# Windowed attention beside a weight projection: units in column order, other load distances, gate stores on ScalarE's queue

## The chip, the cores and the metric

The kernel runs on one core of a Trainium2 chip. The metric is the time on the device in microseconds (us). Five engines work in it: TensorE (PE, with PEld for the loading of the stationary operand), VectorE (DVE), ScalarE (ACT), GpSimd (POOL) and SyncE (SP). DMAs are issued by instructions in the streams of SP, ACT and POOL, and a stream is in order: an instruction that waits holds all behind it.

## The reference

One layer of a hybrid encoder, 1024 tokens (a grid of 16 rows by 64 columns) of 1024 channels, all in float32. What matters here is the middle of it:

```python
h = h + 0.5 * swiglu(rms_norm(h))            # first half of the feed-forward
z = rms_norm(h) @ W_in                       # columns: q | k | v | ssm input | gate_attn | gate_ssm
for every head and every token (r, c):       # attention in a clamped window of 8 rows x 16 columns
    sc = q . k[window] * 64 ** -0.5 + bias[window]
    attn = softmax(sc) @ v[window]
ssm  = bidirectional state-space scan, then a gated linear unit
h = h + (sigmoid(gate_attn) * (attn @ Wa) + sigmoid(gate_ssm) * (ssm @ Ws)) @ W_out
h = h + 0.5 * swiglu(rms_norm(h))            # second half, then an embedding term and a last norm
```

## The kernel before, in words

Every product of float32 matrices is made as three matmuls of high and low parts (`mm3`); `split` makes the parts, the high one with a copy on ScalarE, the low one with a subtraction on VectorE. The large products go by a seven-product scheme of half blocks.

From about 700 us on, after the first feed-forward, the projections of `W_in` are made. Values come first (`values`, results stored to `v_d`), then a loop over `items` (84 of them: twelve column pairs of `W_in`, two for queries and keys in each of four, and eight for gates, seven products each). An item `(n, i)` is four groups of three matmuls (`s_run`), and after each group `tick()` lets a second program advance: the generator `mixer_side()`. So TensorE's order is written out by hand: items, and pieces of the side program between them. The order on the other engines is made by a scheduler from priorities and dependencies.

`s_ahead(n)` loads the weight blocks `LL` items ahead (`s_load`, on ScalarE's queue, line 1506) and makes the operands `LP` = 2 items ahead (`b_operand`, VectorE's sums at line 428 and the split at 159 and 160). `s_evac` (line 1539 and 1543) copies accumulators into `z` tiles or adds to them; `s_out` makes of a finished block either query or key parts (`qkh`, `qkl`, stored by ScalarE's queue to `q_d` and `k_d`) or a gate block, which is stored to `g_d` by GpSimd's queue. The stores are collected in `later` and issued by `s_store` in the next item (line 1549).

The side program's attention is 64 units: eight heads, two halves of the token rows (`rb`), four column blocks (`cb`). In iteration `j` of its loop it makes the scores of unit `j` (`attn_scores`: two matmuls at line 1228, with the query tiles `qh` and `ql` as stationary operand; VectorE adds the bias table `tb`; ScalarE takes the exponential and scales), the transposes of unit `j - 2` (`attn_turn`, line 1244, then `pth` and `ptl`) and the products with the values of unit `j - 4` (`attn_values`, into a PSUM bank `O` that four units share; after the fourth, `ot` at line 1262 goes to `o_d`). Then it yields for three ticks. Two scan steps of the state-space branch go to GpSimd in each iteration (lines 1154 to 1156). All loads of this program are on SP's queue: keys (`load_k`, 1201), queries (`load_q`, 1208), values (`load_v`, 1213), tables (`load_tab`, 1220).

Tiles come from pools with a fixed number of buffers: 24 buffers of 128 x 512 (`tmp`) hold query tiles, `vhl`, `blk`, the parts `wh` and `wl`, `z`, `qkh`, `qkl`, `ot` and `ol` in turn. A new tile waits until the readers of the buffer's former tile are done, a store's landing included. PSUM has eight banks.

After the attention `ssm_out` and the gated unit follow in the side program; `load_br` loads the attention result from `o_d` and splits it for the branch product, and the gates are read back from `g_d` from 1202 us on.

Of the kernel before, what the change touches and what calls it, by code (L numbers as in the profile page):

```python
# [8 lines left out]
F32 = mybir.dt.float32  # L9
# [3 lines left out]
ALU = mybir.AluOpType  # L13
# [28 lines left out]
def encoder_block(ctx, tc, I, out):  # L42
# [1157 lines left out]
        for a, s_ in enumerate(halves2):  # L1200
            nc.sync.dma_start(t[s_].bitcast(F32), k_d[hp, a, halves2[i]])

    def load_q(hd, rb):
        hp, i = hd // 2, hd % 2
        qs[hd, rb] = [tmp("q" + n, dt=F32R) for n in "hl"]
        for a in range(2):
            for s_ in halves2:
                nc.sync.dma_start(qs[hd, rb][a][s_].bitcast(F32), q_d[hp, a, halves2[i], hsl(rb)])

    def load_v(hd, cb):  # L1210
        n = 4 * KNC[cb]
# [10 lines left out]
    def attn_scores(hd, rb, cb):  # L1222
        n = KNC[cb]
        nk = 12 * n
        kv = khl[hd].rearrange("p (r c) -> p r c", c=GRID)[:, 4 * rb:4 * rb + 12, KC0[cb]:KC0[cb] + n]
        s3 = bank("s")[:, 0:nk].rearrange("p (r c) -> p r c", c=n)
        for a in range(2):
            T.matmul(s3, lhsT=qs[hd, rb][a][:, ksl(cb)], rhs=kv, start=a == 0, stop=a == 1)
        sm = ta("sm")[:, 0:nk]
        tab = tabs[2 * hd + rb, KVAR[cb]]  # L1230
        st = ap_.tile([P, 4], F32, tag="stat", bufs=4, name="stat")
        V.tensor_tensor_reduce(out=sm.rearrange("p (r c) -> p r c", c=n), in0=s3,
                               in1=tab.rearrange("p (r c) -> p r c", c=n), scale=-1.0, scalar=3.0e38,
                               op0=ALU.add, op1=ALU.min, accum_out=st[:, 0:1])
        A.activation(sm, sm, AF.Exp, bias=st[:, 0:1], scale=-1.0, accum_out=st[:, 1:2])
        V.reciprocal(st[:, 2:3], st[:, 1:2])
        A.activation(sm, sm, AF.Copy, scale=st[:, 2:3])
        return sm
# [11 lines left out]
    def attn_values(hd, rb, cb, O, ph, pl):  # L1250
        kp = 4 * KNC[cb]
        hl = vld[hd, cb]
        for g in range(3):

            T.matmul(O[:, ksl(cb)], lhsT=hl[0:kp, rb + g], rhs=ph[0:kp, ksl(g)], start=(g == 0), stop=False,
                     skip_group_check=True)
            T.matmul(O[0:64, ksl(cb)], lhsT=hl[0:kp, rb + g, 0:64], rhs=pl[0:kp, ksl(g)], start=False, stop=(g == 2),
                     skip_group_check=True)
        if cb == 3:
            ot, ol = tmp("ot"), tmp("ol")  # L1260
            A.copy(ol[0:64], O[64:128])
            V.tensor_tensor(ot[0:64].rearrange("p (r b c) -> p b r c", r=8, b=4),
                            O[0:64].rearrange("p (b r c) -> p b r c", b=4, r=8),
                            ol[0:64].rearrange("p (b r c) -> p b r c", b=4, r=8), ALU.add)
            late.append((o_d[hd * 64:(hd + 1) * 64, hsl(rb)], ot[0:64]))


    ygs = {}
# [41 lines left out]
    def mixer_side():  # L1310
        yield from u_second()
        while 3 not in stored:
            yield 1
        yield 7
        new_x()
        ld = {}
        for pr in range(3):
            ld[pr] = inject_load(pr)
        yield 10
        for pr in range(NPAIR):  # L1320
            if pr + 3 < NPAIR:
                ld[pr + 3] = inject_load(pr + 3)
            inject(pr, *ld.pop(pr))
            yield 2
        while "v" not in stored:
            scan_steps(1)
            yield 1
        for cb in range(4):
            scan_steps(4)
            yield 4  # L1330
            load_v(0, cb)
        load_tab(0, 0)
        while 0 not in ready:
            scan_steps(1)
            yield 1
        units = [(hd, rb, cb) for hd in range(NH) for rb in range(2) for cb in range(4)]
        n = len(units)
        load_k(0)
        load_q(0, 0)
        for _ in range(6):  # L1340
            scan_steps(1)
            yield 2
        sms, pts, O = {}, {}, {}
        late.clear()
        lo, so = {}, {}
        for j in range(n + 5):
            if j < n:
                hd, rb, cb = units[j]
                b = 2 * hd + rb
                load_tab(b + cb // 2, (1, 2, 0, 0)[cb]) if cb < 3 else None  # L1350
                if cb == 2 and rb == 0:
                    load_q(hd, 1)
                if cb == 2 and rb == 1 and hd + 1 < NH:
                    while hd + 1 not in ready:
                        yield 1
                    load_q(hd + 1, 0)
                if rb == 0 and cb == 2 and hd + 1 in ready:
                    load_k(hd + 1)
                if rb == 1 and cb == 2 and hd + 1 < NH and hd + 1 not in khl:
                    load_k(hd + 1)  # L1360
                sms[j] = attn_scores(hd, rb, cb)
            if 0 <= j - 2 < n:
                pts[j - 2] = attn_turn(units[j - 2][2], sms.pop(j - 2))
            while late:
                nc.scalar.dma_start(*late.pop())
            if 0 <= j - 4 < n:
                hd, rb, cb = units[j - 4]
                if cb == 0:
                    O[hd, rb] = bank("O")
                attn_values(hd, rb, cb, O[hd, rb], *pts.pop(j - 4))  # L1370
                if rb == 1 and hd + 1 < NH:
                    load_v(hd + 1, cb)
            scan_steps(2)
            if j >= n:
                if j - n < 3:
                    lo[j - n] = ssm_load(j - n)
            yield 3
        scan_steps(NCH)
        for p in range(NPAIR + 1):
            if 3 <= p + 3 < NPAIR:  # L1380
                lo[p + 3] = ssm_load(p + 3)
            if p < NPAIR:
                so[p] = ssm_out(p, *lo.pop(p))
            if p > 0:
                so.pop(p - 1)()
            yield 1 + p % 2
        yield 3
        glu_load(0)
        raws = [glu_raw(0), glu_raw(1)]
        yield 11  # L1390
        glu_act(0)
        glu_load(1)
        yield 2
        glu_act(1)
        for t in range(2):
            yield from glu_half(t, raws)
# [61 lines left out]
    def load_br(t, b):  # L1458

        res = []  # L1460
        if b == 0:
            for k in range(0, 4, 2):
                st = tst("br")
                nc.sync.dma_start(st.rearrange("p (k c) -> p k c", k=2),
                                  o_d[k * P:(k + 2) * P, hsl(t)].rearrange("(k p) c -> p k c", p=P))
                for i in range(2):
                    hi, lo = tx("bh"), tx("bl")
                    split(hi, lo, st[:, hsl(i)])
                    res.append((hi, lo))
            return res  # L1470
        for k in range(4):
            st = tmp("br")
            hi, lo = tx("bh"), tx("bl")
            mark["br"] = nc.sync.dma_start(st.rearrange("p (s c) -> p s c", s=L),
                                           y2_d[ksl(k)].rearrange("p (s c) -> p s c", s=L)[:, :, t * 64:(t + 1) * 64]).ins
            sv = st.rearrange("p (s c) -> p c s", s=L)
            hv, lv = (x.rearrange("p (c s) -> p c s", s=L) for x in (hi, lo))
            split(hv, lv, sv)
            res.append((hi, lo))
        return res  # L1480
# [30 lines left out]
    def s_out(n, c, t, second, src):  # L1511
        kind, m = pairs[n]
        if kind == "g":
            if c == "21":
                z, src = tmp("z21"), src
                A.copy(z, src)
                src = z
            later.append((nc.gpsimd, g_d[2 * m + second, :, hsl(t)], src))
            return
        hi, lo = tmp("qkh", dt=F32R), tmp("qkl", dt=F32R)  # L1520
        if second:
            A.activation(hi, src, AF.Copy, scale=0.125)
            V.scalar_tensor_tensor(lo, src, 0.125, hi.bitcast(F32), ALU.mult, ALU.subtract)
        else:
            def view(x):
                return x.rearrange("p (b r c) -> p r b c", b=4, r=8)
            sv = src.rearrange("p (r b c) -> p r b c", r=8, b=4)
            A.copy(view(hi), sv)
            V.tensor_tensor(view(lo), sv, view(hi).bitcast(F32), ALU.subtract)
        for i, x in enumerate((hi, lo)):  # L1530
            later.append((nc.scalar, (k_d if second else q_d)[m, i, :, hsl(t)], x.bitcast(F32)))
# [32 lines left out]
        with tc.high_priority(offset=PRI):  # L1564
            s_evac(n, i)

    LL, LP = 5, 2
    done_ = {"l": 0, "p": 0}

    def s_ahead(n):  # L1570
# [387 lines left out]
```

## Time and profile before

| what | value |
|---|---|
| median of three runs | 2112.91 us (2112.85 to 2114.22) |
| the profiled execution | 2113.88 us |
| its span, first to last instruction | 2112.1 us |
| mean granted clock | 0.992 |
| busy: PE, DVE, ACT, POOL | 2060.9, 1468.4, 1011.0, 480.2 us |
| the 64 attention units | 825.4 to 1061.9 us |

In a row of the timeline stand start, length, engine, line, operation, the tiles written and read by the program's names, and in brackets the idle time before it on its engine and what ended it. SPq, ACTq and POOLq are the DMA issues in those engines' streams; their length is the issue and not the transfer. A row of waits reads: who waited, for what, total us, times, longest. The granted clock is TensorE's as a share of full speed.

### The profile page before, as it was taken

The page shows a single profiled execution, that of the slowest core. Times are in us where ns is not written, and L with a number is a line of the kernel's source. Part 1 is how long each engine was busy: PE and PEld are TensorE (multiplying, and loading weights), DVE is VectorE, ACT ScalarE, POOL GpSimd, SP SyncE. Part 2 cuts the span into 40 slices and gives each one's busy share as a digit, 9 for nine tenths or more (in the row PEclk, how much of TensorE's full clock was granted, in tenths as well). Part 3 has the DMA queues.
Part 4 walks back from the last instruction along what each step waited for, and adds up shares of the span by engine and source line. Part 5 has one row for each costly group of instructions (what it writes and reads, how often), then busy time and mean ns, then how long its engine had stood idle before and what let it go on. Part 6 is the DMA issues. An engine that isn't in the chain of part 4 may idle for free.

```text
span 2112.1 us, 28243 instructions
## 1 busy us (share of the span) xinstructions
PE 2060.9 (98%) x9518; PEld 1685.9 (80%) x9518; DVE 1468.4 (70%) x2478; ACT 1011.0 (48%) x1878; POOL 480.2 (23%) x720
## 2 busy tenths in 40 slices
PE   9999999999999998898999999999999999999998
PEld 3788888888888887777888788788888888888887
DVE  7897776667967847555655669896565665785855
ACT  6434333344445535656655546553333334445544
POOL 0037565540000518888031002000000000000000
PEclk9999999999999999999999999999999999999999
DMA  3434444485543557566675776143323338533302
GB/s 131 142 118 152 129 131 128 139 284 156 185 120 107 149 180 238 171 197 192 192 243 185 231 264 164 65 154 102 123 80 121 99 100 293 170 105 95 115 26 80
DMA packets 212464, 319.75 MB, mean 151 GB/s; under 512 B 37856, under 2 KB 81504, under 8 KB 212320
## 3 DMA queue, kind: packets, MB, share of 16 engines
q1 hardware_dynamic: 173840, 258.14, 38.9%
q10 hardware_dynamic: 31760, 44.07, 6.3%
q0 software_dynamic: 6720, 15.75, 2.6%
q8 instruction: 75, 1.23, 0.2%
q14 instruction: 69, 0.57, 0.1%
HBM read 224.01 MB, written 93.85 MB: 150 GB/s over the span
## 4 chain that ended last, share of the span: by engine, by line
PE 80%; POOL 7%; DVE 5%; DMA 3%; ACT 2%; issue 2%; SPq 0%; ACTq 0%; DVEq 0%; POOLq 0%
PE dx L190 4%; PE dx L191 4%; PE dx L192 4%; PE gx L190 3%; PE ux L190 3%; PE ux L192 3%; PE gx L192 3%; PE gx L191 3%; PE ux L191 3%; POOL sc L1154 3%; PE dy L192 2%; PE dy L190 2%; PE dy L191 2%; POOL X L1156 2%; POOL sc L1155 2%
## 5 line engine op out<-in xcount | busy, mean ns | idle before, releaser
L159 ACT CAST wh<-hbuf 128x512 fp32r<-128x512 f32 x280 | 173.0, 622 | 389.2 <-PE gx L191 84.3
L160 DVE TENSOR_TENSOR wl<-hbuf,wh 128x512 fp32r<-128x512 f32 x280 | 215.4, 772 | 121.7 <-ACT wh L159 119.7
L159 ACT CAST wh<-wblk 128x512 fp32r<-128x512 f32 x190 | 117.9, 622 | 188.7 <-PE dx L191 82.4
L160 DVE TENSOR_TENSOR wl<-wblk,wh 128x512 fp32r<-128x512 f32 x190 | 130.6, 690 | 49.8 <-ACT wh L159 40.2
L190 PE MATMUL dx<-ah,wh 128*128 128x512 f32 x416 | 163.5, 393 | 0.4 <-DVE hbuf L694 0.3
L192 PE MATMUL dx<-ah,wl 128*128 128x512 f32 x416 | 161.9, 389 | 0.0
L191 PE MATMUL dx<-al,wh 128*128 128x512 f32 x416 | 161.9, 389 | 0.0
L160 DVE TENSOR_TENSOR al<-araw,ah 128x512 fp32r<-128x512 f32 x154 | 106.5, 696 | 49.6 <-PE dx L191 21.1
L190 PE MATMUL gx<-xh,wh 128*128 128x512 f32 x320 | 125.0, 391 | 1.3 <-DVE c L581 1.2
L190 PE MATMUL ux<-xh,wh 128*128 128x512 f32 x320 | 125.0, 390 | 0.0
L191 PE MATMUL gx<-xl,wh 128*128 128x512 f32 x320 | 124.5, 389 | 0.0
L192 PE MATMUL ux<-xh,wl 128*128 128x512 f32 x320 | 124.5, 389 | 0.0
L192 PE MATMUL gx<-xh,wl 128*128 128x512 f32 x320 | 124.5, 389 | 0.0
L191 PE MATMUL ux<-xl,wh 128*128 128x512 f32 x320 | 124.5, 389 | 0.0
L159 ACT CAST ah<-araw 128x512 fp32r<-128x512 f32 x154 | 94.9, 619 | 44.5 <-PE dx L191 14.2
L160 DVE TENSOR_TENSOR wl<-blk,wh 128x512 fp32r<-128x512 f32 x84 | 61.4, 733 | 49.6 <-ACT wh L159 47.2
L190 PEld LDWEIGHTS dx<-ah,wh 128*128 128x128 f32 x416 | 78.1, 188 | 18.6 <-DVE hbuf L694 1.2
L191 PEld LDWEIGHTS dx<-al,wh 128*128 128x128 f32 x416 | 78.1, 188 | 16.8 <-issue 0.7
L428 DVE TENSOR_TENSOR hbuf<-hbuf 128x512 f32<-128x512 f32 x120 | 89.7, 749 | 2.1
L192 PEld LDWEIGHTS dx<-ah,wl 128*128 128x128 f32 x416 | 78.1, 188 | 16.3
L1154 POOL TENSOR_TENSOR sc<-X,rho 128x128 f32<-128x128 f32 x128 | 75.5, 590 | 59.4 <-ACT X L1137 49.6
L190 PE MATMUL px<-xh,wh 128*128 128x512 f32 x192 | 80.6, 420 | 6.1 <-ACT z L1539 4.7
(399 smaller groups left out, 5775.6 us busy)
## 6 DMA issues: line engine op xcount, KB each, us to landing
araw<-a_d SPq DMA_DIRECT2D x154, 256.0 KB
a_d<-c SPq DMA_DIRECT2D x148, 256.0 KB
wblk<-in_wd SPq DMA_DIRECT2D x88, 256.0 KB
hbuf<-in_wg SPq DMA_DIRECT2D x40, 512.0 KB
hbuf<-in_wu SPq DMA_DIRECT2D x40, 512.0 KB
blk<-in_win ACTq DMA_DIRECT2D x48, 256.0 KB
hbuf<-in_xT SPq DMA_DIRECT2D x32, 256.0 KB
h_d<-hbuf ACTq DMA_DIRECT2D x32, 256.0 KB
```

The costliest lines, as they stand in the source:

```text
L159: A.copy(hi, src)
L160: return eng.tensor_tensor(lo, src, hi.bitcast(F32), ALU.subtract)
L190: T.matmul(o, lhsT=wh, rhs=xh, start=first, stop=False, skip_group_check=more)
L191: T.matmul(o, lhsT=wh, rhs=xl, start=False, stop=False, skip_group_check=more)
L192: T.matmul(o, lhsT=wl, rhs=xh, start=False, stop=last, skip_group_check=more)
L428: V.tensor_tensor(b11, (b12, b22, None, None, b21)[i - 2], b11, ALU.subtract)
L1154: G.tensor_tensor(sc, both, rho4, ALU.mult)
L1155: G.tensor_tensor(cross1, cross1, cross, ALU.add)
L1156: G.tensor_tensor(x1, sc[:, 0], x1, ALU.add)
```

## The change

The units run in the order head, column block, row half, so that both row halves of a column block follow each other and share the value tile. With it:

- A query tile holds a column pair `cp` of both row halves instead of one row half with all columns; its two runs per partition are 1 KB each instead of one of 2 KB. It is loaded at `u == 1` and `u == 5` of the eight units of a head, three units ahead of its first use; before, two.
- Tables are loaded two units ahead, and three of them ahead of the loop. Keys are asked for where they were, at the third and seventh unit of a head.
- Two value tiles are loaded ahead of the loop, and each further one two column blocks (four units) ahead; before, the four of a head were loaded a whole head ahead.
- The bank `O` holds a head and a column pair; `ot` is written in the bank's own order with no strided view, `o_d` keeps that order within a row half, and the split in `load_br` reorders it with the strided view that `ot` had.
- Gate stores go by `nc.scalar` instead of `nc.gpsimd`.
- `LL` goes from 5 to 4, so weight blocks are loaded four items ahead instead of five.

The numbers of matmuls and of DMAs stay the same.

```diff
-    def load_q(hd, rb):
+    def load_q(hd, cp):
...
-                nc.sync.dma_start(qs[hd, rb][a][s_].bitcast(F32), q_d[hp, a, halves2[i], hsl(rb)])
+                nc.sync.dma_start(qs[hd, cp][a][s_].rearrange("p (t c) -> p t c", t=2).bitcast(F32),
+                                  q_d[hp, a, halves2[i]].rearrange("p (t b c) -> p t b c", t=2, b=2)[:, :, cp])
...
-            T.matmul(s3, lhsT=qs[hd, rb][a][:, ksl(cb)], rhs=kv, start=a == 0, stop=a == 1)
+            T.matmul(s3, lhsT=qs[hd, cb // 2][a][:, ksl(2 * rb + cb % 2)], rhs=kv, start=a == 0, stop=a == 1)
...
-        if cb == 3:
+        if cb % 2 == 1 and rb == 1:
             ot, ol = tmp("ot"), tmp("ol")
             A.copy(ol[0:64], O[64:128])
-            V.tensor_tensor(ot[0:64].rearrange("p (r b c) -> p b r c", r=8, b=4),
-                            O[0:64].rearrange("p (b r c) -> p b r c", b=4, r=8),
-                            ol[0:64].rearrange("p (b r c) -> p b r c", b=4, r=8), ALU.add)
-            late.append((o_d[hd * 64:(hd + 1) * 64, hsl(rb)], ot[0:64]))
+            V.tensor_tensor(ot[0:64], O[0:64], ol[0:64], ALU.add)
+            late.append((o_d[hd * 64:(hd + 1) * 64].rearrange("p (t b c) -> p t b c", t=2, b=2)[:, :, cb // 2],
+                         ot[0:64].rearrange("p (t c) -> p t c", t=2)))
...
-            load_v(0, cb)
+            if cb < 2:
+                load_v(0, cb)
         load_tab(0, 0)
+        load_tab(1, 0)
...
-        units = [(hd, rb, cb) for hd in range(NH) for rb in range(2) for cb in range(4)]
+        units = [(hd, rb, cb) for hd in range(NH) for cb in range(4) for rb in range(2)]
...
-                b = 2 * hd + rb
-                load_tab(b + cb // 2, (1, 2, 0, 0)[cb]) if cb < 3 else None
-                if cb == 2 and rb == 0:
+                u = j % 8
+                if u not in (2, 3):
+                    load_tab(2 * ((j + 2) // 8) + j % 2, KVAR[(j + 2) % 8 // 2])
+                if u == 1:
                     load_q(hd, 1)
-                if cb == 2 and rb == 1 and hd + 1 < NH:
+                if u == 5 and hd + 1 < NH:
                     while hd + 1 not in ready:
                         yield 1
                     load_q(hd + 1, 0)
-                if rb == 0 and cb == 2 and hd + 1 in ready:
+                if u == 2 and hd + 1 in ready:
                     load_k(hd + 1)
-                if rb == 1 and cb == 2 and hd + 1 < NH and hd + 1 not in khl:
+                if u == 6 and hd + 1 < NH and hd + 1 not in khl:
                     load_k(hd + 1)
...
-                attn_values(hd, rb, cb, O[hd, rb], *pts.pop(j - 4))
-                if rb == 1 and hd + 1 < NH:
-                    load_v(hd + 1, cb)
+                attn_values(hd, rb, cb, O[hd], *pts.pop(j - 4))
+                if rb == 1 and (j - 4) // 2 + 2 < 4 * NH:
+                    load_v(((j - 4) // 2 + 2) // 4, ((j - 4) // 2 + 2) % 4)
...
-                    split(hi, lo, st[:, hsl(i)])
+                    sv = st[:, hsl(i)].rearrange("p (b r c) -> p b r c", b=4, r=8)
+                    hv, lv = (x.rearrange("p (r b c) -> p b r c", r=8, b=4) for x in (hi, lo))
+                    split(hv, lv, sv)
...
-            later.append((nc.gpsimd, g_d[2 * m + second, :, hsl(t)], src))
+            later.append((nc.scalar, g_d[2 * m + second, :, hsl(t)], src))
...
-    LL, LP = 5, 2
+    LL, LP = 4, 2
```

The order that comes of it, at three places. First GpSimd's stream of before, where the first gate block, `z12`, is stored among the scan steps (`sc` and `X` are the scan's tiles):

```order
L1154 TENSOR_TENSOR sc_6135<-X_6590,rho_1128 128x128
L1155 TENSOR_TENSOR sc_6135<-sc_6135 128x64
L1156 TENSOR_TENSOR X_6590<-sc_6135,X_6590 128x32x2
L1549 DMA g_d_85<-z12_7910 128x512
L1154 TENSOR_TENSOR sc_6135<-X_6590,rho_1128 128x128
L1155 TENSOR_TENSOR sc_6135<-sc_6135 128x64
```

And the same store in ScalarE's stream of the changed kernel (`blk` is a weight block, `sm` a softmax, `pth` its transpose):

```order
L1545 COPY z12_7910<-px_7716 128x512
L1512 DMA blk_7912<-in_win 128x512
L159 CAST wh_7914<-blk_7765 128x512
L1369 DMA o_d_84<-ot_7898 128x1x256
L1236 ACTIVATE sm_7932,stat_7933<-sm_7932,stat_7933 128x288
L1247 CAST pth_7942<-pt_7938 96x384
L1512 DMA blk_7964<-in_win 128x512
L159 CAST wh_7967<-blk_7515 128x512
L1238 ACTIVATE sm_7932<-sm_7932,stat_7933 128x288
L1555 DMA g_d_85<-z12_7910 128x512
L1247 CAST pth_7998<-pt_7994 96x384
```

The store has left the scan's stream; it now stands nine rows behind the copy that begins its block, with a split, an exponential and transposes of the attention around it.

Second ScalarE's stream at the start of the items, behind the last value stores, before:

```order
L1549 DMA v_d_80<-vs_7132 128x4x128
L1506 DMA blk_7151<-in_win 128x512
L159 CAST wh_7154<-blk_6845 128x512
L159 CAST xh_7189<-s3_7143 128x512
L1539 COPY z11_7183<-px_7158 128x512
L159 CAST wh_7185<-blk_6849 128x512
```

And in the changed kernel:

```order
L1555 DMA v_d_80<-vs_7132 128x4x128
L159 CAST wh_7152<-blk_6845 128x512
L159 CAST xh_7189<-s3_7143 128x512
L1545 COPY z11_7181<-px_7156 128x512
L1512 DMA blk_7183<-in_win 128x512
L159 CAST wh_7185<-blk_7028 128x512
```

The block load has moved from ahead of the first evacuation `z11` to behind it; the cast `wh` still stands ahead.

Third SP's stream at the query load of the 25th unit (the first of head 3; its query tile is `qh_8651` before and `qh_8593` after; `khl_8857` and `khl_8853` are the key tile of head 4), before:

```order
L1213 DMA vhl_8514<-v_d_80 96x1x512
L1220 DMA tb_8543<-in_tabs 128x384
L1220 DMA tb_8595<-in_tabs 128x288
L1220 DMA tb_8649<-in_tabs 128x288
L1201 DMA khl_8857<-k_d_82 64x1024
L1208 DMA qh_8651<-q_d_81 64x512 x2
L1208 DMA ql_8652<-q_d_81 64x512 x2
```

And in the changed kernel:

```order
L1214 DMA vhl_8508<-v_d_80 128x1x512
L1221 DMA tb_8591<-in_tabs 128x288
L1208 DMA qh_8593<-q_d_81 64x2x256 x2
L1208 DMA ql_8594<-q_d_81 64x2x256 x2
L1214 DMA vhl_8622<-v_d_80 128x1x512
L1221 DMA tb_8651<-in_tabs 128x288
L1201 DMA khl_8853<-k_d_82 64x1024
```

The query load has moved ahead of that key load, with a value load ahead of it that stood elsewhere before.

More of the change, by code (lines that the diff above doesn't have):

```diff
@@ L1201, in load_k @@
             nc.sync.dma_start(t[s_].bitcast(F32), k_d[hp, a, halves2[i]])
-    def load_q(hd, rb):
+    def load_q(hd, cp):
         hp, i = hd // 2, hd % 2
-        qs[hd, rb] = [tmp("q" + n, dt=F32R) for n in "hl"]
+        qs[hd, cp] = [tmp("q" + n, dt=F32R) for n in "hl"]
         for a in range(2):
             for s_ in halves2:
-                nc.sync.dma_start(qs[hd, rb][a][s_].bitcast(F32), q_d[hp, a, halves2[i], hsl(rb)])
+                nc.sync.dma_start(qs[hd, cp][a][s_].rearrange("p (t c) -> p t c", t=2).bitcast(F32),
+                                  q_d[hp, a, halves2[i]].rearrange("p (t b c) -> p t b c", t=2, b=2)[:, :, cp])
     def load_v(hd, cb):
@@ L1252, in attn_values @@
         hl = vld[hd, cb]
+        oc = ksl(2 * rb + cb % 2)
         for g in range(3):
-            T.matmul(O[:, ksl(cb)], lhsT=hl[0:kp, rb + g], rhs=ph[0:kp, ksl(g)], start=(g == 0), stop=False,
+            T.matmul(O[:, oc], lhsT=hl[0:kp, rb + g], rhs=ph[0:kp, ksl(g)], start=(g == 0), stop=False,
                      skip_group_check=True)
-            T.matmul(O[0:64, ksl(cb)], lhsT=hl[0:kp, rb + g, 0:64], rhs=pl[0:kp, ksl(g)], start=False, stop=(g == 2),
+            T.matmul(O[0:64, oc], lhsT=hl[0:kp, rb + g, 0:64], rhs=pl[0:kp, ksl(g)], start=False, stop=(g == 2),
                      skip_group_check=True)
-        if cb == 3:
+        if cb % 2 == 1 and rb == 1:
             ot, ol = tmp("ot"), tmp("ol")
             A.copy(ol[0:64], O[64:128])
-            V.tensor_tensor(ot[0:64].rearrange("p (r b c) -> p b r c", r=8, b=4),
-                            O[0:64].rearrange("p (b r c) -> p b r c", b=4, r=8),
-                            ol[0:64].rearrange("p (b r c) -> p b r c", b=4, r=8), ALU.add)
-            late.append((o_d[hd * 64:(hd + 1) * 64, hsl(rb)], ot[0:64]))
+            V.tensor_tensor(ot[0:64], O[0:64], ol[0:64], ALU.add)
+            late.append((o_d[hd * 64:(hd + 1) * 64].rearrange("p (t b c) -> p t b c", t=2, b=2)[:, :, cb // 2],
+                         ot[0:64].rearrange("p (t c) -> p t c", t=2)))
     ygs = {}
@@ L1367, in mixer_side @@
                 hd, rb, cb = units[j - 4]
-                if cb == 0:
-                    O[hd, rb] = bank("O")
-                attn_values(hd, rb, cb, O[hd, rb], *pts.pop(j - 4))
-                if rb == 1 and hd + 1 < NH:
-                    load_v(hd + 1, cb)
+                if cb % 2 == 0 and rb == 0:
+                    O[hd] = bank("O")
+                attn_values(hd, rb, cb, O[hd], *pts.pop(j - 4))
+                if rb == 1 and (j - 4) // 2 + 2 < 4 * NH:
+                    load_v(((j - 4) // 2 + 2) // 4, ((j - 4) // 2 + 2) % 4)
             scan_steps(2)
```

## The prediction

> **What bounds the kernel now.** I read the page first, then a table of engine time by stage, the waits of the attention stage, TensorE's timeline in it, and last the queues that feed it. The page's span and engine row, then the table's row for the attention stage (columns: length; busy time and count of PE, PEld, DVE, ACT, POOL; granted clock; DMA share; GB/s):
>
> ```profile
> span 2112.1 us, 28243 instructions
> PE 2060.9 (98%) x9518; PEld 1685.9 (80%) x9518; DVE 1468.4 (70%) x2478; ACT 1011.0 (48%) x1878; POOL 480.2 (23%) x720
> ...
> 796.00:1062.00 266.00, 241.75 (x1348) 205.27 (x1349) 167.90 (x398) 163.75 (x369) 184.25 (x367) 0.95 0.64 193
> ```
>
> TensorE is busy 98% of the span, so only its idle time and its slow-clock time can be won. Both are in this stage: 266.0 − 241.8 = 24.2 us idle and a granted clock of 0.95, with every other engine below 70% and the DMA engines at 64%. What TensorE, VectorE and the SP queue wait for there, from the list of waits (total us, times, longest):
>
> ```profile
> DVE blk L428 <- DMA blk<-in_win: 11.7, 6, 3.8
> DVE ot L1262 <- DMA g_d<-z: 9.2, 1, 9.2
> PE s L1228 <- DMA qh<-q_d: 8.7, 5, 2.7
> PE s L1228 <- DMA ql<-q_d: 8.4, 7, 3.4
> PE pt L1244 <- ACT sm L1237: 5.5, 1, 5.5
> PE px L190 <- ACT z L1539: 4.7, 3, 3.2
> ...
> SPq L1208 <- DMA g_d<-z: 25.6, 3, 14.7
> SPq L1201 <- DMA k_d<-qkh: 14.3, 3, 8.8
> ```
>
> TensorE waits for query tiles (8.7 + 8.4 = 17.1 us), for one softmax (5.5) and for accumulator evacuations (4.7). The SP queue, which loads the queries, waits three times for gate stores to land. The holes stand in short windows, and in each of them the clock is low too (columns as above):
>
> ```profile
> 792.00:800.00 8.00, 4.82 (x15) 3.60 (x14) 4.76 (x7) 4.70 (x9) 7.06 (x13) 0.79 0.89 291
> 862.00:878.00 16.00, 10.27 (x47) 8.33 (x46) 5.39 (x14) 5.56 (x15) 14.14 (x29) 0.79 0.33 108
> 896.00:906.00 10.00, 7.53 (x34) 5.95 (x32) 4.88 (x11) 4.78 (x11) 8.51 (x20) 0.83 0.59 199
> 914.00:922.00 8.00, 5.50 (x23) 4.33 (x22) 3.24 (x9) 3.99 (x10) 6.82 (x16) 0.79 0.77 222
> 957.00:971.00 14.00, 7.96 (x34) 6.40 (x33) 4.96 (x13) 5.80 (x14) 11.80 (x29) 0.76 0.54 168
> 992.00:1001.00 9.00, 6.08 (x25) 4.74 (x24) 3.90 (x12) 6.15 (x14) 7.54 (x18) 0.81 0.52 170
> ```
>
> The time lost to the clock is (1 − clock) × length: 1.7 us at 792, 3.4 at 862, 1.7 at 896, 1.7 at 914, 3.4 at 957, 1.7 at 992. TensorE's holes and, for the pace, its first and last score row in the stage, from its timeline (start, length, instruction, idle time before it and what ended that):
>
> ```profile
> 796.03 0.80 PE L190 MATMUL px<-xh,wh 128*128 128x512 f32 x1 [3.18 <-ACT z L1539]
> ...
> 825.42 0.29 PE L1228 MATMUL s<-khl,qh 128*128 128x288 f32 x1
> 827.00 0.40 PE L1228 MATMUL s<-khl,ql 128*128 128x288 f32 x1 [1.28 <-DMA ql<-q_d]
> 872.61 0.45 PE L1244 MATMUL pt<-ident,sm 128*96 128x128 f32 x1 [5.47 <-ACT sm L1237]
> 884.77 0.37 PE L1228 MATMUL s<-khl,ql 128*128 128x288 f32 x1 [0.23 <-DMA ql<-q_d]
> 917.13 0.37 PE L1228 MATMUL s<-khl,qh 128*128 128x288 f32 x1 [1.90 <-DMA qh<-q_d]
> 918.10 0.37 PE L1228 MATMUL s<-khl,ql 128*128 128x288 f32 x1 [0.61 <-DMA ql<-q_d]
> 961.31 0.37 PE L1228 MATMUL s<-khl,qh 128*128 128x288 f32 x1 [2.69 <-DMA qh<-q_d]
> 965.02 0.58 PE L1228 MATMUL s<-khl,ql 128*128 128x288 f32 x1 [3.35 <-DMA ql<-q_d]
> 1061.89 0.29 PE L1228 MATMUL s<-khl,qh 128*128 128x288 f32 x1
> ```
>
> Sixty-four units in 1061.9 − 825.4 = 236.5 us are 3.75 us a unit; an item of the weight projections is four ticks and a unit three, so an item takes 5.0 us.
>
> **The change part by part.** All sums are made against the profiled execution, 2113.9 us, which stands 1.0 us above the median of 2112.9.
>
> *Gate stores from GpSimd's queue to ScalarE's.* One store followed from its data to its victims, from the timelines of four engines, and the landing times of all 32 of them:
>
> ```profile
> 852.04 0.69 DVE L1543 TENSOR_TENSOR z<-py,z 128x512 f32<-128x512 f32 x1
> 868.39 0.58 POOL L1549 DMA_DIRECT2D g_d<-z  x1
> 870.80 0.68 DVE L1262 TENSOR_TENSOR ot<-O,ol 64x512 f32<-64x512 f32 x1 [9.20 <-DMA g_d<-z]
> 879.74 1.13 SPq L1208 DMA_DIRECT2D qh<-q_d  x2
> ...
> 953.73 1.48 SPq L1208 DMA_DIRECT2D qh<-q_d  x2
> 961.04 1.08 SPq L1208 DMA_DIRECT2D ql<-q_d  x2
> DMA to landing us min/median/max: 2.3/4.4/6.9
> ```
>
> The gate block was ready at 852.04 + 0.69 = 852.7, but its store was issued at 868.4, 15.7 us later, because GpSimd had scan steps ahead of it; the transfer took about 2.3 us. VectorE's `ot` needed that buffer and stood for 9.20 us with the softmax of the next units queued behind it; that is TensorE's 5.47 us hole at 872.6. The SP queue also waited 14.7 us for a gate store and could not issue the query loads behind it, which gave the 0.23 at 884.8; near 954 the same happened again, and the query loads at 953.7 and 961.0 came so late that TensorE idled 2.69 and 3.35 us. Sum: 5.47 + 0.23 + 2.69 + 3.35 = 11.7 us idle and 3.4 + 3.4 = 6.8 us of clock, 18.5 us in all. On ScalarE a store stands some nine instructions of 0.3 to 0.6 us behind its data. I take −16.7 and leave 1.8 for one store that still lands late; the bounds are −11.7 (holes alone) and −18.5.
>
> The clock loss is put to the holes because it stands in their windows, also after small ones: 1.90 + 0.61 us at 917 were followed by 0.79. The Trainium skill, "TensorE: Matmul & The Clock Gate", section "Why this matters for your kernels", warns of gaps above about 3 us alone; the window at 914 shows the loss with less, so the trace decides against it here. By the page the losses at 896, 914 and 992 would not go with the holes, and the sum would be 2.6 us smaller.
>
> *Queries three units ahead, by column pair.* TensorE's remaining query waits are 17.1 − 6.3 (0.23 + 2.69 + 3.35) − 1.28 (the first unit, whose load is not moved) = 9.5 us, and the clock at 896, 914 and 992 another 5.1: 14.6 us at most. In the order the loads for the hole at 917 no longer stand behind the next head's key load, which waited up to 8.8 us for its stores; that hole (2.51 + 1.7) should go. Elsewhere the loads gain about one unit, 3.75 us, but they also have a values or table load ahead of them that wasn't there. I take half, −7.3; bounds −4.2 and −14.6. Each load now has 1-KB runs in place of 2-KB ones; with the DMA engines at 64% I cost this at nothing.
>
> *The hole at 796.* ScalarE's cast ahead of the evacuation waited for value stores and the block load stood ahead of it:
>
> ```profile
> 794.35 0.62 ACT L159 CAST wh<-blk 128x512 fp32r<-128x512 f32 x1 [3.03 <-DMA v_d<-vs]
> ```
>
> With LL at 4 the block load falls behind the evacuation, but this cast and its wait stay ahead. Of 3.18 + 1.7 = 4.9 us I take −1.0; bounds 0 and −4.9.
>
> *Weight blocks one item later.* VectorE already waited 11.7 us for blocks, in six places; the longest, from ScalarE's issue to VectorE's use, and for scale one pass of the softmax (the group's mean is in ns):
>
> ```profile
> 1017.57 0.33 ACTq L1506 DMA_DIRECT2D blk<-in_win  x1
> 1024.09 0.69 DVE L428 TENSOR_TENSOR blk<-blk 128x512 f32<-128x512 f32 x1 [3.80 <-DMA blk<-in_win]
> ...
> L1235 ACT ACTIVATE sm<-sm,stat 128x288 f32<-128x288 f32 x32 | 17.2, 537 | 7.5 <-DVE stat L1232 5.7 <-DVE qkl L1523 1.2 <-issue 0.4
> ```
>
> None of these reached TensorE. A stall of VectorE delays the softmax queued behind it, and a transpose comes two units (7.5 us) after its scores; with some 3 us for the softmax itself (four passes of about 537 ns and their hand-overs, an estimate from that row) the cover is about 4.5 us. If each wait grew by the whole 5.0 us, the longest would overshoot by 3.8 + 5.0 − 4.5 = 4.3 us and the other five, 1.6 us on average now, by 2.1 each: 14.8 us. If the loads land in time, nothing. I take +3.0, near the lower end, since the nearest row, 3.80, showed nothing on TensorE.
>
> *The rest.* ScalarE gets 32 more issues of 0.33 us (10.6 us over some 320 us, beside an engine 62% busy), and anything that waits there holds its casts and exponentials. Values come two column units ahead in place of a whole head; even the shorter lead, about 8.6 us of matmuls in the order, is above the gate stores' landings of 2.3 to 6.9. Together +1.5; bounds 0 and +6. The 16-element runs move from `ot` to the splits of the attention branch. The rows of one form:
>
> ```profile
> L159 ACT CAST bh<-br 128x512 fp32r<-128x512 f32 x16 | 12.9, 871 | 9.0 <-DMA br<-o_d 9.0
> L1528 ACT CAST qkh<-z 128x512 fp32r<-128x512 f32 x4 | 2.5, 616 | 2.0 <-DVE z L1543 2.0
> ```
>
> The key and query split already has that access pattern and takes 616 ns on ScalarE, so the moved one costs nothing that TensorE sees. Table loads two units ahead and the order of the units change no count; zero, with the query term's bounds for doubt.
>
> Sum: −16.7 − 7.3 − 1.0 + 3.0 + 1.5 = −20.5, so 2093.4 on the profiled scale and **2092.4** on that of the median.
>
> **The rivals.** *Everything comes back*: 18.5 + 14.6 + 2.5 (half of the hole at 796) less 1.5 gives 2112.9 − 34.1 = 2078.8. For it: the new order gives each query load about the same lead. Against: tables, values, keys and queries still share SP's queue.
>
> *The transfers, not the issue, are what is late*: the stores move at an earlier time into the query and block loads, and buffers come free no sooner. Then the first term is nothing and the sum is −7.3 − 1.0 + 4.5 = −3.8, 2109.1. Against it stands 2.3 us of transfer beside 15.7 of waiting for issue. For it: the windows at 792 and 914 show DMA shares of 0.89 and 0.77. The Trainium skill, "DMA: Bandwidth & Descriptors", section "Issuing engines are not separate DMA queues", says that the transfers of all issuing engines interleave on the same DMA engines and another queue saves issue time alone; by that rule this rival would hold wherever issue time was not the loss.
>
> *Slower by the blocks*: the stage has about 266 / 5.0 = 53 items, so 30 block loads at four in seven items. If half stall VectorE 2.1 us beyond the cover and seven of those holes bring a clock loss of 1.7, the cost is 15 × 2.1 + 7 × 1.7 = 43.4 in place of 3.0: 2132.8. It decides against the change once blocks cost about 24 us more than I give, an overshoot of 1.6 us in fifteen places with no clock loss. For it: waits of up to 3.8 us at the old lead. Against: only six of thirty waited at all.
>
> **How the numbers follow.** My forecast has 0.60, full recovery 0.13, late transfers 0.15, blocks 0.12. With the bounds of its terms the forecast's own range is 2083 to 2103. About 0.2%, 4.2 us, is what a measurement of this kernel can tell from no change: 2108.7 is the bound of faster, and late transfers straddle it, so half of their chance and a little more is put to faster: 0.60 + 0.13 + 0.08 = 0.81; the other 0.07 is no change, and blocks are slower, 0.12. The range runs from 2079, which cuts off half of full recovery, to 2110, which leaves out the blocks and the upper edge of late transfers: 0.06 + 0.12 + 0.02.
>
> **What would show it.** In the new profile: SP's waits for `g_d` at L1208 gone and no `ot` waiting for `g_d` (first term); TensorE's waits for `qh` and `ql` below 6 us in all (second); the px hole near 796 still there (third); VectorE's block waits at 15 to 25 us with no TensorE hole behind them (fourth); clock of the stage near 0.98. The prediction is wrong if gate stores on ScalarE's queue stand as long for their data or buffers as on GpSimd's, if the query waits stay at 9 us, or if TensorE's transposes begin to wait for softmax in many places.

## The result, and the profile after

The changed kernel takes 2098.75 us (median of five, 2093.88 to 2104.60) against 2112.91 (2112.82 to 2114.79): ratio 0.9935, 95% interval 0.9913 to 0.9957. That is 14.2 us faster by the medians, where 20.5 were forecast; 2092.4 was predicted, with a range of 2079 to 2110. The runs of the changed kernel spread over 10.7 us, those of before over 2.

The page after, and two rows of the table by stage, the attention stage and what follows it:

```profile
span 2097.0 us, 28186 instructions
PE 2057.4 (98%) x9518; PEld 1681.4 (80%) x9518; DVE 1468.5 (70%) x2478; ACT 1010.1 (48%) x1878; POOL 465.2 (22%) x688
...
796.00:1062.00 266.00, 252.80 (x1462) 214.59 (x1463) 180.46 (x422) 172.88 (x393) 178.60 (x354) 0.99 0.71 209
1062.00:1260.00 198.00, 191.75 (x907) 158.98 (x906) 114.06 (x188) 109.34 (x194) 22.60 (x36) 0.97 0.73 235
```

The second of these rows before:

```profile
1062.00:1260.00 198.00, 191.79 (x956) 160.32 (x955) 114.86 (x195) 110.53 (x201) 29.91 (x50) 1.00 0.73 237
```

The span is 15.1 us shorter. TensorE is busy 2060.9 − 2057.4 = 3.5 us less, as less of its work ran at the low clock, and so idle 11.6 us less. The gain is in the attention stage: in the same 266 us TensorE is busy for 252.8 us instead of 241.8, at a clock of 0.99 instead of 0.95. Behind the stage it went the other way: from 1062 to 1260 the clock was 1.00 before and is 0.97 after.

The waits of that stage after the change:

```profile
DVE blk L428 <- DMA blk<-in_win: 24.2, 10, 4.9
DVE blk L430 <- DMA blk<-in_win: 6.8, 5, 2.1
PE O L1257 <- DMA vhl<-v_d: 5.5, 3, 2.1
PE px L190 <- ACT z L1545: 3.5, 3, 2.1
PE pt L1245 <- ACT sm L1238: 2.8, 4, 1.8
PE py L190 <- ACT z L1545: 1.8, 1, 1.8
PE s L1229 <- DMA ql<-q_d: 1.3, 1, 1.3
...
SPq L1221 <- PE pt L1245: 45.3, 15, 5.3
SPq L1208 <- DMA g_d<-z: 4.9, 3, 3.5
```

The query waits fell from 17.1 to 1.3 us, and those 1.3 are the first unit's. No `ot` waits for a gate store any more. Two waits are new on TensorE: values (5.5) and an evacuation on the other accumulator (1.8). Behind them two others grew: VectorE's for weight blocks, from 11.7 to 24.2 at line 428 and from 0.5 to 6.8 at line 430, and one on SP's queue that before's list has not got: table loads that wait for a transpose, 45.3 us in fifteen places, which reads as a wait for one of the small buffers that tables, softmaxes and transposes share. Before, table loads waited too, but for other things. By kind of load, the waits of SP's queue in the stage were and are: tables 43.1 and 75.3 us, queries 72.4 and 46.1, values 27.6 and 15.0, keys 33.6 and 22.8. Query loads still wait for gate stores, but 4.9 us in place of 25.6.

The same first gate block as in the prediction, from its data to its store:

```profile
851.99 0.67 DVE L1549 TENSOR_TENSOR z<-py,z 128x512 f32<-128x512 f32 x1
852.69 0.33 ACTq L1555 DMA_DIRECT2D g_d<-z  x1
```

It is ready at 852.66 and issued at 852.69; before, 15.7 us lay between. What TensorE's holes look like now, with the chain of one of them, from the timelines of VectorE, ScalarE and TensorE, ahead of it the issue of the block that it waits for:

```profile
933.13 0.37 ACTq L1512 DMA_DIRECT2D blk<-in_win  x1
941.03 0.82 DVE L428 TENSOR_TENSOR blk<-blk 128x512 f32<-128x512 f32 x1 [4.86 <-DMA blk<-in_win]
942.24 0.15 DVE L1237 RECIPROCAL stat<-stat 128x1 f32<-128x1 f32 x1
942.42 0.54 ACT L1238 ACTIVATE sm<-sm,stat 128x288 f32<-128x288 f32 x1 [6.07 <-DVE stat L1237]
943.01 0.31 PE L1245 MATMUL pt<-ident,sm 128*96 128x128 f32 x1 [1.82 <-ACT sm L1238]
```

A block load issued at 933.1 is used at 941.0. VectorE stands 4.86 us for it, the reciprocal of a softmax is queued behind it, ScalarE stands 6.07 us for that, and TensorE 1.82. The other kind, a value tile, on SP's queue and on TensorE:

```profile
954.26 3.89 SPq L1221 DMA_DIRECT2D tb<-in_tabs  x2
961.58 0.48 SPq L1201 DMA_DIRECT2D khl<-k_d  x1
962.16 1.00 SPq L1221 DMA_DIRECT2D tb<-in_tabs  x1
963.22 0.67 SPq L1214 DMA_DIRECT2D vhl<-v_d  x1
...
970.16 0.33 PE L1257 MATMUL O<-pth,vhl 96*128 96x128 f32 x1 [2.07 <-DMA vhl<-v_d]
```

The value load stood on SP's queue behind tables and a key load and was issued at 963.2, 4.9 us before TensorE came to it; TensorE could go on 6.9 us after the issue. The two longest waits of SP's queue from 950 to 964:

```profile
SPq L1201 <- DMA k_d<-qkh: 3.4, 1, 3.4
SPq L1221 <- DMA k_d<-qkl: 3.2, 1, 3.2
```

Just ahead of this value load it was key stores, not transposes, that held the queue.

### The profile page after: what moved, and what is told of

Its sections match the earlier page's. It is cut to its first block, busy times and chain, and to the rows that moved or that the text cites. A ratio compares the mean times of both kernels' runs of the same rounds, so it can differ in the third digit from the quotient of the medians.

```text
span 2097.0 us, 28186 instructions
## 1 busy us (share of the span) xinstructions
PE 2057.4 (98%) x9518; PEld 1681.4 (80%) x9518; DVE 1468.5 (70%) x2478; ACT 1010.1 (48%) x1878; POOL 465.2 (22%) x688
## 4 chain that ended last, share of the span: by engine, by line
PE 81%; DMA 6%; DVE 6%; ACT 3%; POOL 2%; issue 1%; SPq 1%; ACTq 0%; DVEq 0%
PE dx L190 4%; PE dx L191 4%; PE dx L192 4%; PE ux L190 3%; PE gx L190 3%; PE ux L191 3%; PE ux L192 3%; PE gx L191 3%; PE gx L192 3%; PE dy L192 2%; PE dy L190 2%; PE dy L191 2%; DMA blk<-in_win 2%; PE uy L190 2%; PE gy L190 2%; PE gy L192 2%
## 5 line engine op out<-in xcount | busy, mean ns | idle before, releaser
L160 DVE TENSOR_TENSOR al<-araw,ah 128x512 fp32r<-128x512 f32 x154 | 106.7, 697 | 51.2 <-PE dx L191 21.1
L159 ACT CAST ah<-araw 128x512 fp32r<-128x512 f32 x154 | 95.0, 619 | 46.7 <-PE dx L191 14.2
L1154 POOL TENSOR_TENSOR sc<-X,rho 128x128 f32<-128x128 f32 x128 | 79.7, 623 | 58.9 <-ACT X L1137 48.9
L191 PEld LDWEIGHTS dx<-al,wh 128*128 128x128 f32 x416 | 78.1, 188 | 16.7 <-issue 0.7
```

Of the source, the lines that this page charges most:

```text
L159: A.copy(hi, src)
L160: return eng.tensor_tensor(lo, src, hi.bitcast(F32), ALU.subtract)
L191: T.matmul(o, lhsT=wh, rhs=xl, start=False, stop=False, skip_group_check=more)
L1154: G.tensor_tensor(sc, both, rho4, ALU.mult)
```

## The experiments

Two theories. **G**: the late issue of the gate stores was most of the loss (−16.7 of −20.5 in the forecast). **Q**: the earlier query loads carry the gain and a late gate store does no harm. Each kernel was timed five times or more, beside the kernel before on the same chip; medians, and ratios with 95% intervals. The kernel before itself had medians of 2111.7 to 2113.8 in these groups. The waits shown are those of one execution of each kernel. Two executions of the changed kernel give a scale for them: 24.2 and, in `e8_change_again`, 21.1 us of block waits at line 428, 5.5 and 4.2 of value waits, 2.8 and 3.9 of softmax waits. The profiled execution is the slowest of its group in `e4_values3` and `e6_before_queries3`, and the fastest in `e1_gates_back`, `e2_gates_alone`, `e7_queries3_gates`, `e8_change_again`, `e10_blocks6` and `e13_change_blocks6`.

### Gate stores alone, and all but the gate stores

`e2_gates_alone`, the kernel before with

```diff
-            later.append((nc.gpsimd, g_d[2 * m + second, :, hsl(t)], src))
+            later.append((nc.scalar, g_d[2 * m + second, :, hsl(t)], src))
```

> The kernel before with only its gate stores moved to ScalarE's queue. Theory G: 2095 to 2101 us; the holes at 872, 961 and 965 (11.7 us) gone with 3 to 5 us of slow clock, the other query waits (9.5 us) still there. Theory Q: 2109 to 2114 us, as the query loads still come two units ahead and behind key loads, and other waits fill the place of the three holes.

Measured: 2098.81 us, ratio 0.9927 (0.9914 to 0.9940). The waits:

```profile
DVE blk L428 <- DMA blk<-in_win: 15.0, 8, 3.2
PE s L1228 <- DMA ql<-q_d: 5.2, 7, 1.4
PE s L1228 <- DMA qh<-q_d: 3.9, 3, 1.8
```

The two big holes are gone, 9.1 us of query waits are left. One line of the change gives all of the gain that can be measured: theory G, and theory Q is out as it was put. `e1_gates_back` undoes that line alone in the changed kernel.

> The changed kernel with its gate stores back on GpSimd's queue, nothing else undone. Theory G (the gate stores' late issue carries most of the gain, as forecast: 16.7 of 20.5 us): most of the 14.2 us goes, 2107 to 2114 us, and the profile again shows ot or the SP queue's query loads waiting 7 to 15 us for g_d, with TensorE holes of 3 to 6 us behind them. Theory Q (the query loads' earlier place carries it, a gate store may be late without harm): 2096 to 2102 us, TensorE's query waits below 3 us, and the g_d landings late but with nobody waiting for them on the path.

Measured: 2104.02 us, ratio 0.9953 (0.9941 to 0.9965); between the two theories' ranges. Gate stores are late again, but others wait for them:

```profile
DVE blk L428 <- DMA blk<-in_win: 19.7, 9, 4.0
DVE wl L160 <- DMA g_d<-z: 13.6, 4, 5.2
...
SPq L1208 <- DMA g_d<-z: 13.0, 2, 7.2
```

No `ot` waits for `g_d`. Query loads do, on SP's queue, 13.0 us in two places, but TensorE waits for queries only 2.1 us in all; the low part `wl` of a weight waits in four places of 5.2 us at most. So the rest of the change is worth about 10 us as long as the stores are late, and nothing that could be measured once they are early (0.9935 against 0.9927): the two halves remove much the same loss. That the rest does it by holding fewer value tiles in the shared buffers is argued, not shown.

### Late issue, or the kind of queue

The line changes the queue and the moment of issue at once. `e9_no_scan` leaves the stores on GpSimd's queue and takes the scan away ahead of them:

```diff
-            G.tensor_tensor(sc, both, rho4, ALU.mult)
-            G.tensor_tensor(cross1, cross1, cross, ALU.add)
-            G.tensor_tensor(x1, sc[:, 0], x1, ALU.add)
```

> The kernel before without the scan's three GpSimd operations a step (the state-space scan is left out, so its branch carries only what is injected); gate stores stay on GpSimd's queue, which then has nothing ahead of them. If the late issue behind the scan steps is what cost time (theory G as the forecast told it): g_d stores issued within 1 to 3 us of their data, the two softmax and query holes gone, 2096 to 2101 us as with the gate stores alone. If it is the kind of queue that makes the stores slow: the holes stay in part, 2106 to 2113 us.

Measured: 2095.40 us, ratio 0.9923 (0.9909 to 0.9937). The first store, and the landing times of all:

```profile
853.33 0.68 DVE L1540 TENSOR_TENSOR z<-py,z 128x512 f32<-128x512 f32 x1
854.31 0.56 POOL L1546 DMA_DIRECT2D g_d<-z  x1 [122.96 <-DVE stat L1233]
...
DMA to landing us min/median/max: 2.3/4.7/7.1
```

Ready at 854.0, issued at 854.3, and they land in 4.7 us at the median, against 4.4 before. Same queue, much the same landing, and the same gain as with the other queue (just below the range that was expected). Leaving out the scan does one thing more: with GpSimd busy 10.2 us of the stage in place of 184.3, VectorE's `wl` takes 687 ns in place of 752. The gate stores alone gave the same gain with the scan in place and `wl` at 762. What the two runs have in common is the early issue: the wait for it was the loss.

### How far ahead the queries are loaded

`e6_before_queries3` is the kernel before with the query loads one unit earlier:

```diff
-                if cb == 2 and rb == 0:
+                if cb == 1 and rb == 0:
                     load_q(hd, 1)
-                if cb == 2 and rb == 1 and hd + 1 < NH:
+                if cb == 1 and rb == 1 and hd + 1 < NH:
```

> The kernel before with its queries three units ahead and nothing else, gate stores still on GpSimd's queue. Theory G: the two holes behind late gate stores (5.47 us at 872; 2.69 and 3.35 at 961) need the stores, so 2107 to 2112 us, a gain of 2 to 6 us from the other query waits. Theory Q: one unit of 3.75 us covers holes that are at most 3.4 us long, so all but the softmax hole go: 2099 to 2104 us.

Measured: 2107.61 us, ratio 0.9980 (0.9971 to 0.9988), as G expects. Its waits, and the two large holes in TensorE's timeline:

```profile
PE pt L1244 <- ACT sm L1237: 19.2, 6, 6.4
DVE ot L1262 <- DMA g_d<-z: 9.5, 1, 9.5
...
874.97 0.88 PE L1244 MATMUL pt<-ident,sm 128*96 128x128 f32 x3 [6.31 <-ACT sm L1237]
942.32 0.47 PE L1244 MATMUL pt<-ident,sm 128*128 128x128 f32 x1 [6.38 <-ACT sm L1237]
```

TensorE no longer waits for a query at all, yet only 4 us are won: the late gate stores now reach it through the softmax, 19.2 us instead of 5.5. The hole at 875 stands behind VectorE's 9.5 us wait for `g_d`, those at 942 and 1013 (3.0 us) behind two waits of ScalarE's cast `wh` for it, 7.4 and 7.0 us. Waits for evacuations grew as well, from 4.7 to 10.1 us; 4.4 of that stand behind a block wait. `e5_queries2` takes the earlier load out of the changed kernel (`u == 2` and `u == 6`).

> The changed kernel with the queries two units ahead again (loaded at the third and seventh unit of a head). Theory G (the gate stores carry the gain; the later query load only opens small holes): 2099 to 2105 us, with 2 to 6 us of TensorE query waits back, as in the run with the gate stores alone. Theory Q (the query lead carries much of what is won): 2106 to 2112 us, with query waits near 10 us.

Measured: 2099.49 us, ratio 0.9946 (0.9933 to 0.9959), with 8.0 us of query waits (6.7 + 1.3, the longest 3.8). `e8_change_again` is the changed kernel on the same chip:

> The changed kernel once more, on the same chip as the three others, since its runs spread over 10 us: 2094 to 2105 us, median 2098 to 2101. If the spread comes of the waits' chance timing, it is found again; every theory expects the same here.

Measured: 2096.88 us, 2093.91 to 2103.32, ratio 0.9935 (0.9921 to 0.9949): the spread is there again. By the medians the third unit of lead is worth 2.6 us in the changed kernel; the intervals overlap, so it may be nothing.

### Blocks, values and buffers

`e3_blocks5` sets `LL` back to 5 in the changed kernel, `e4_values3` loads the values three column blocks ahead:

```diff
-    LL, LP = 4, 2
+    LL, LP = 5, 2
```

```diff
-                if rb == 1 and (j - 4) // 2 + 2 < 4 * NH:
-                    load_v(((j - 4) // 2 + 2) // 4, ((j - 4) // 2 + 2) % 4)
+                if rb == 1 and (j - 4) // 2 + 3 < 4 * NH:
+                    load_v(((j - 4) // 2 + 3) // 4, ((j - 4) // 2 + 3) % 4)
```

(the second with three value tiles loaded ahead of the loop).

> The changed kernel with the weight blocks five items ahead again. VectorE's waits for blocks rose from 11.7 to 24.2 us (line 428) and TensorE now waits for evacuations and softmax in places (about 5.7 us of holes between 850 and 964). Theory B (the blocks' shorter lead costs what the forecast put at 3 us, or somewhat more): 2091 to 2096 us and block waits near 12 us. Rival (buffers are the limit: one block more held takes a buffer from queries and values, whose loads then come later): 2099 to 2106 us, with query or value waits of TensorE growing by more than the block waits shrink.

Measured: 2097.75 us, ratio 0.9922 (0.9910 to 0.9934).

> The changed kernel with the values three column blocks ahead instead of two. TensorE waits for value tiles three times in the changed kernel (2.07, 1.41 and 2.04 us at 968 to 1000), which the forecast held for covered. If the lead is too short: these holes go and the time falls by 4 to 8 us, to 2091 to 2095. If the loads are late because SP's queue waits for buffers or stores, one more tile held moves the wait elsewhere: 2097 to 2104, with value or query waits still there.

Measured: 2095.47 us, ratio 0.9915 (0.9900 to 0.9930). First the two main waits of the run with five items, then those of the run with values further ahead:

```profile
DVE blk L428 <- DMA blk<-in_win: 23.9, 9, 6.9
PE O L1257 <- DMA vhl<-v_d: 8.2, 6, 2.3
```

```profile
DVE blk L428 <- DMA blk<-in_win: 26.5, 11, 4.5
PE pt L1245 <- ACT sm L1238: 13.8, 13, 2.1
```

Five items leave VectorE's block waits at line 428 where they were; those at line 430 (6.8 us) go, and the value waits of TensorE grow from 5.5 to 8.2: a wait seems exchanged for another. With values earlier TensorE waits for none of them, but for the softmax 13.8 us in place of 2.8, in an execution 6.8 us above that kernel's median. Neither median can be told from the changed kernel's.

`e7_queries3_gates` joins the two edits that work in before's order (the diffs of `e2_gates_alone` and `e6_before_queries3`).

> The kernel before with queries three units ahead and gate stores on ScalarE's queue, but units, values, tables and LL as before. If the two add (the 9.1 us of query waits that the gate stores alone left go too, nothing new comes): 2088 to 2093 us, faster than the change. If what the queries gain is lost to block and value waits, as in the change: 2095 to 2101 us, with the query waits gone and VectorE's block waits above 20 us.

Measured: 2094.92 us, ratio 0.9920 (0.9908 to 0.9933): query waits gone, 23.8 us of block waits, 6.0 us of softmax holes, no value waits on TensorE. The second expectation came true in its waits for queries and blocks; the time lies just below its range. On top of it `e10_blocks6` sets `LL` to 6, and `e12_buffers25` gives 25 large buffers and 11 small ones in place of 24 and 12.

> The fastest version so far (before, queries three units ahead, gate stores on ScalarE's queue) with the weight blocks six items ahead. VectorE waits there 23.8 us for blocks, and each of TensorE's softmax holes (6.0 us) stands behind such a wait. If the distance in items sets when a block comes: 2088 to 2093 us and block waits below 15 us. If the free buffer sets it, as the run with five items instead of four suggests: 2094 to 2098 us, block waits unchanged at 20 to 26 us.

> The same fastest version with 25 buffers of 128 x 512 instead of 24, and 11 of the small ones instead of 12 to make room. If the free buffer sets when blocks come: block waits fall to 12 to 20 us, 2090 to 2094 us. If ScalarE's in-order stream or the transfers set it: no change, 2094 to 2098 us; if the eleven small buffers (tables, softmaxes, transposes) are one too few, TensorE's softmax waits grow and it is 2096 to 2104 us.

Measured: 2093.07 us, ratio 0.9902 (0.9890 to 0.9915), and 2094.72 us, 0.9923 (0.9908 to 0.9939). The run with six items:

```profile
DVE sm L1232 <- DMA tb<-in_tabs: 22.8, 13, 3.6
PE pt L1244 <- ACT sm L1237: 1.5, 4, 0.6
DVE blk L428 <- DMA blk<-in_win: 1.2, 2, 0.9
```

The block waits fell from 23.8 to 1.2 us and the softmax holes from 6.0 to 1.5: here the distance was what was short, not the buffers; one large buffer more (and one small one less) left 20.7 us of block waits. VectorE's waits did not vanish, though: it now waits 22.8 us for tables, where it waited 6.6, and these waits, none above 3.6 us, leave TensorE hardly a hole. I had leaned the other way after the run with five items. This is the fastest version measured, about 20 us below before; its interval all but clears that of the gate stores alone (0.9915 against 0.9914) and that of the changed kernel (0.9913). `e13_change_blocks6` puts six items into the changed kernel.

> The changed kernel with the weight blocks six items ahead instead of four. In the order of before, six items took VectorE's block waits from 23.8 to 1.2 us; in the changed one, five left them at 23.9. If the distance is what is short and only has to be long enough: block waits below 5 us, TensorE's softmax holes gone, 2090 to 2095 us. If the changed order holds too many tiles for that (values and tables then come late in their place): 2096 to 2102 us, with value waits of TensorE above 5 us.

Measured: 2095.82 us, ratio 0.9919 (0.9904 to 0.9935):

```profile
PE O L1257 <- DMA vhl<-v_d: 5.1, 6, 1.5
PE pt L1245 <- ACT sm L1238: 1.9, 1, 1.9
DVE blk L428 <- DMA blk<-in_win: 1.3, 2, 0.7
```

The block waits go here too (1.3 us), between the two expectations: TensorE's value waits stay, and SP's table loads still wait 39.4 us for transposes. Whether this version is faster than the change as given stays open; the intervals overlap.

## Why the prediction was right, and where its terms were off

**Direction, mechanism and main term held.** The gate stores were forecast at −16.7 on the profiled scale; alone they measured 0.9927, about −15 us, and this run and the one without the scan together show that the late issue was the reason. The row that carried this was a ready time of 852.7 against an issue at 868.4. The rival of late transfers falls with the run without the scan: there the stores land as slowly as before (medians of 4.7 and 4.4 us) and the two large holes are gone. The gain is this term's alone: the other four were forecast at −3.8 together, and the step from the gate stores alone to the whole change, 0.9927 to 0.9935, can't be told from nothing. The Trainium skill, "DMA: Bandwidth & Descriptors", section "Issuing engines are not separate DMA queues", says that issuing from several engines saves only the time it takes to start a DMA, usually a small one. Here that time was not small: a store stood 15.7 us behind other work in an in-order stream. What it says of the transfers no run here shows, as the profiles have no landing times for ScalarE's queue.

**The clock part of that term was priced too high.** Busy time fell by only 3.5 us over the whole kernel, where the gate stores' term had 5.0 of clock and the queries' up to 5.1. Low clock times the whole window counts time in which TensorE was idle anyway: at 862 the window lost 3.4 us by that formula, but the clock was low from about 870.6 on and the hole lasted to 872.6; with the like at 962, some 2 of the 6.8 us are idle time counted as clock too (an estimate from windows of 2 us). More of it came back elsewhere. Apart from the last few us of the kernel, which are slow in both, all slow periods of before lie between 792 and 1001, 13.6 us by the formula. After, they come to 6.8 us: one of 1.7 is in the stage (877 to 887), and 5.1 us lie behind it, where the forecast put no cost, 1.7 from 1108 to 1118 and 3.4 in the window of this row:

```profile
1172.00:1184.00 12.00, 9.88 (x30) 7.38 (x29) 9.36 (x10) 9.23 (x10) 0.00 (x0) 0.72 0.06 22
```

**The query term was the step that failed in size.** It was put at −7.3, as if the two terms added. The waits did go (17.1 to 1.3 us, better than the forecast's below 6), but the time did not follow: −4 us when tried alone, and 0.9927 to 0.9920, some 1.5 us and no measurable difference, on top of the early gate stores. What took its place is seen in the waits: the softmax behind VectorE's block waits (6.0 us with both edits in before's order), and in the changed order values (5.5).

**Block loads: the mechanism was right, the cover too large.** Block waits of 15 to 25 us were forecast; 24.2 came at line 428, the line that the forecast had read, and 31.0 with line 430. They came with holes behind them, which the forecast denied. The sign of failure that it named, softmax waits of the transposes in many places, came only in part: four places, 2.8 us. The cover was put at 4.5 us; the chain at 941 shows 4.86 us of stall becoming 1.82 of hole, a cover of 3.0 in this one chain. The shorter `LL` was not all of it: with the gate stores alone and `LL` at 5 the same waits were 15.0, with the queries earlier too 23.8. With `LL` back at 5 in the changed kernel they were 23.9. Why earlier query loads lengthen them (a stage that asks for its blocks sooner, or fewer free buffers) is not shown.

**Values and tables were the terms missed.** Values were taken as covered, with 8.6 us of lead against landings of up to 6.9. The lead in the order was not the lead in time: on SP's queue the value load shown was issued 4.9 us before use, behind loads that waited for key stores. Table loads were costed at zero; their waits grew from 43.1 to 75.3 us, 45.3 of them for transposes, a row that before hasn't got. How much of the value holes is owed to those is not shown. The medians fall 6.3 us short of the forecast. The value holes, 5.5 us, and the slow clock behind the stage, 5.1, are each near that size, and no run separates them; the run with values earlier had no value holes and was not measurably faster.

**The smaller steps.** The hole at 796 stayed, 2.15 us instead of 3.18, as forecast. The clock of the stage came to 0.99 against a forecast of 0.98. The moved splits cost nothing that can be seen: their casts take 862 ns against 871. TensorE's longest wait for them is 2.12 us against 1.67, and behind it stands the slow period at 1172, where before had none. That is not owed to the move: with the gate stores alone, splits unmoved, the wait is 2.30 us and the clock of that stage 0.99. The rows after:

```profile
L159 ACT CAST bh<-br 128x512 fp32r<-128x512 f32 x16 | 12.8, 862 | 6.4 <-DMA br<-o_d 6.4
...
1174.41 0.79 PE L190 MATMUL br<-bh,wh 128*128 128x512 f32 x1 [2.12 <-ACT bh L159]
```

Two figures of the forecast are worked out in no line of it: the lead of 8.6 us for the values, and its own range of 2083 to 2103. The bounds of its five terms, added up, give 2074.9 to 2117.8.

## What to carry to other kernels

When a store is late, look first at the instruction that issues it: if its data were ready long before and other work of that engine stands between, move the issue to an engine whose stream is not full; here that one line gave all of the gain that could be measured. Waits that share a cause do not add up: take one away and measure before counting the next. A lead counted in the program's order is only a lead in time if nothing ahead in the same queue waits.

## What the runs showed of the hardware that was not expected

The low clock does not follow each hole of a given length. In the changed kernel's profile a hole of 1.85 us at 877 was followed by a clock of 0.83 in its window, while holes of 2.07 us at 968 and 1.41 us at 977 left it at 1.00:

```profile
877.00:887.00 10.00, 8.15 (x41) 6.99 (x41) 6.41 (x18) 7.37 (x18) 8.51 (x20) 0.83 0.76 193
...
962.00:980.00 18.00, 14.07 (x82) 11.49 (x82) 12.11 (x31) 12.17 (x28) 15.59 (x31) 1.00 0.71 217
```

Even the same hole need not bring it twice. Here is one place of the changed kernel in its two profiled executions, with the window around it; first the one after the change, then `e8_change_again`:

```profile
1111.77 0.50 PE L190 MATMUL glu<-yh,wgl 128*128 128x512 f32 x1 [1.65 <-ACT yh L159]
1108.00:1118.00 10.00, 8.12 (x28) 6.09 (x27) 4.12 (x7) 4.88 (x10) 0.00 (x0) 0.83 0.48 157
...
1108.73 0.50 PE L190 MATMUL glu<-yh,wgl 128*128 128x512 f32 x1 [1.65 <-ACT yh L159]
1105.00:1115.00 10.00, 8.12 (x35) 6.15 (x34) 4.61 (x7) 4.89 (x9) 0.00 (x0) 1.00 0.45 155
```

The hole is 1.65 us both times, and TensorE is busy 8.12 of 10 us both times; 28 matmuls are counted in the one and 35 in the other. So a price of clock per hole, as the prediction had it, can only be good on the average; why one hole brings it and a longer one doesn't, no run here tells. The Trainium skill, "TensorE: Matmul & The Clock Gate", section "Why this matters for your kernels", warns of gaps above about 3 us; the loss at 877 came below that. The clock also has a part in the spread of the changed kernel's runs, some 10 us where before has 2 to 7.5 in a group: the two profiled executions span 2097.0 and 2092.1 us, and 4.3 us of that difference are TensorE's busy time (2057.4 and 2053.1). That the rest of the spread has the same cause is not shown.
